# Two-layer encoder on one core: A's q features split once on 128 rows and put together by copies, V of B and C split for four heads at once, a reciprocal square root in ten steps

## The chip, the cores and the metric

The kernel runs on one core of a Trainium2 chip. The core has five engines with a program each: TensorE (PE) multiplies, VectorE (DVE) and ScalarE (ACT) work elementwise, GpSimd (POOL) helps VectorE, and SyncE (SP) does little but issue transfers. They meet by semaphores, and each runs its own program in order. The metric is the device time of one execution in microseconds (us). Results of matmuls go to PSUM, which has eight banks here, each 512 floats wide on 128 partitions; everything else lies in SBUF.

## What is computed

x is 512 tokens by 1024 features, in float32. Each of two layers does this (cut down from the reference):

```python
h = _rms_norm(x, ln1_g[l])
(a_q, a_k, a_v, b_q, b_k, b_v, c_cq, c_ckv, c_kr, gate_logits) = _split_columns(h @ w_in[l])
y_a = _gqa_axial(a_q, a_k, a_v, ...)      # A: 8 query heads, 2 key heads, 64 wide, axial rotary
y_b = _diff_attention(b_q, b_k, b_v, ...) # B: 8 heads, difference of two softmaxes, V 64 wide
y_c = _mla(c_cq, c_ckv, c_kr, ...)        # C: 8 heads from ranks 384 and 256, V 64 wide
merged = sum(sigmoid(gate_logits[n]) * (y[n] @ w_branch[l, n]) for n in range(3))
x = x + merged @ w_out[l]
x = x + relu(_rms_norm(x, ln2_g[l]) @ w_ff1[l]) ** 2 @ w_ff2[l]
```

and a last `_rms_norm` follows. In A, q and k are normalised head by head before the rotary step. In C the V of all heads is the second half of `c_kv @ w_ukv`.

## The kernel before

**Numbers in two parts.** Every operand of a matmul is held as a rounded part, *hi*, and the rest, *lo*, so that a product is two or three matmuls. `split` makes such a pair: ACT copies the source to hi (`hi`, L224), and DVE takes the source minus hi (`lo`, L227). For weights, ACT's cast gives `wh` (L61) and DVE or POOL the rest, `wl` (L67).

**Places.** Most intermediate tiles come from one pool of 25 equal SBUF places (`s4`, L201; NS4, L1233), 4 KB a partition each. A tile holds its place until the last instruction that reads it is done, and the next tile of the pool waits for that. PSUM is shared out (L1234): two banks S for scores, two T for transposes, one V for the products with V, and three L for everything else, among them `tm` (projections with tokens on the partitions), `gate` and `br`.

**Order.** `plan` writes a layer as a list of items with an estimated cost each; `weave` mixes the items of an attention with items that only need PE, and `run` (L167) goes through the list. Steps behind an item are put off by a given lag (`defer`, L147). A scheduler then lays the instructions out on the engines. SP's queue carries all the weight loads (`wr`, two buffers), in order, and the small copies in SBUF.

**The parts that the change touches.** All stand on the path of a layer in this order.

- `rsqrt` (L241): a reciprocal square root on DVE, from a bit trick and two rounds of refinement, in eleven small operations. It is called 24 times: for the norms, for A's q (`a_R`) and k (`rs`, in front of `a_kr`), for B's outputs, for C's ranks, and at the end of the kernel (`rf`, in front of `dg` and `bc`, L377).
- `a_q` (L496): a group g of four q heads. `late` (L519) transposes two heads at a time into a T bank, 128 rows by 512 tokens, and makes of it a tile `a_G` in which the first head has hi on rows 0 to 63 and lo on rows 64 to 127 of plane 0, and the second head hi on rows 64 to 127 and lo on rows 0 to 63 of plane 1. ACT writes two hi's of 64 rows, DVE two lo's of 64 rows, each half into its place. B's first transposes (`tp<-ident,b_t`) use the same two T banks.
- `v_evac` (L460), called from `b_v` (L707) and `c_v` (L905): a row tile `tt` of a projection (128 tokens, four heads of 64) comes from an L bank and is split for two heads at a time, by two calls, into two tiles; each of these holds all four row tiles of one pair of heads. A head's turn in the attention reads one such tile (`vt`, L752 and L961). `c_v(1)`, for heads 4 to 7, is woven into the heads 2 and 3 of C's attention.
- `c_pair` (L915): ACT writes q's hi into two planes by two operations of 64 by 512.
- `gate_branch` (L966): `gate` is 24 matmuls into an L bank and then DVE's `gz` (L983), which frees it; `br` is 12 into an L bank and then a DVE operation (L993 or L995).

Of the kernel before, what the change touches and what calls it, by code (L numbers as in the profile page):

```python
# [141 lines left out]
class Trunk:  # L142
    def __init__(self, tc, a, depth):
        self.tc, self.nc, self.a, self.depth = tc, tc.nc, a, depth
# [96 lines left out]
    def rsqrt(self, dst, v, n):  # L241
        v_ = self.nc.vector
        y, t, h = (self.small(f"rs{c}", n) for c in "yth")
        v_.tensor_scalar(y.bitcast(I32), v.bitcast(I32), 1, None, op0=ALU.logical_shift_right)
        v_.tensor_scalar(h, v, -0.5, None, op0=ALU.mult)
# [3 lines left out]
        v_.tensor_tensor(t, t, h, op=ALU.mult)  # L249
        v_.scalar_tensor_tensor(y, t, 1.5, y, op0=ALU.add, op1=ALU.mult)  # L250
        v_.tensor_tensor(t, y, y, op=ALU.mult)
        v_.tensor_tensor(t, t, h, op=ALU.mult)
# [207 lines left out]
    def v_evac(self, vt, tt, ps, scale):  # L460

        v = vt[:, tt].rearrange("p (a b) -> p a b", b=64)
        s = ps.rearrange("p (a b) -> p a b", b=64)
        self.hi(v[:, 0::3], s, 1.0 if scale is None else scale)
        self.lo(v[:, 1:3], s, v[:, 0::3], scale)
# [30 lines left out]
    def a_q(self, l, g):  # L496
# [22 lines left out]
        def late():  # L519
            for j in range(2):  # L520
                T = self.transpose4(st["r"], slice(j * 128, (j + 1) * 128))
                G = self.s4("a_G")
                self.hi(G[0:64, 0], T[0:64])
                self.hi(G[64:128, 1], T[64:128])
                self.lo(G[64:128, 0], T[0:64], G[0:64, 0])
                self.lo(G[0:64, 1], T[64:128], G[64:128, 1])
                self.aG[2 * g + j] = G
# [179 lines left out]
    def b_v(self, l, hb):  # L707
        def evac(tt, ps):
            if tt == 0:
                for j in range(2):  # L710
                    self.bV[2 * hb + j] = self.s4("b_V", (128, 4, 256))
            for j in range(2):
                self.v_evac(self.bV[2 * hb + j], tt, ps[:, j * 128 : (j + 1) * 128], self.rstd[:, tt : tt + 1])
# [15 lines left out]
    def att_b(self, l):  # L729
# [20 lines left out]
        def vt(h):  # L750
            o = 128 * (h % 2)
            return lambda k: self.bV[h // 2][:, k, o : o + 128]  # L752
# [152 lines left out]
    def c_v(self, l, hb):  # L905
        def evac(tt, ps):
            if tt == 0:
                for j in range(2):
                    self.cV[2 * hb + j] = self.s4("c_V", (128, 4, 256))
            for j in range(2):  # L910
                self.v_evac(self.cV[2 * hb + j], tt, ps[:, j * 128 : (j + 1) * 128], None)
# [3 lines left out]
    def c_pair(self, l, j):  # L915
# [5 lines left out]
        def q():  # L921
            ps = self.ps("L", "uq")
            self.mm(ps, self.fm_pairs(w, 0, self.want(self.cf, "q")))
            for e in range(2):
                Q = self.s4("c_Q")
                r, o = (slice(0, 64), slice(64, 128)) if e == 0 else (slice(64, 128), slice(0, 64))
                self.hi(Q[r, 0], ps[r])
                self.hi(Q[r, 1], ps[r])
# [21 lines left out]
    def att_c(self):  # L950
# [8 lines left out]
        def vt(h):  # L959
            o = 128 * (h % 2)  # L960
            return lambda k: self.cV[h // 2][:, k, o : o + 128]  # L961
# [414 lines left out]
```

## Time and profile before

| | |
|---|---|
| three runs | 1872.10, 1874.61, 1874.87 us; median 1874.61 |
| the profiled execution | 1872.25 us |
| its span, first to last instruction | 1870.4 us |
| granted clock of PE, mean | 0.993 |
| ACT, `hi` of `a_G`, 64 by 512 | 0.59 us, 16 times |
| DVE, `lo` of `a_G`, 64 by 512 | 0.69 us, 16 times |
| ACT and DVE, `b_V`, 128 by 128 | 0.37 and 0.34 us, 32 times each |
| ACT and DVE, `c_V`, 128 by 128 | 0.28 and 0.28 us, 32 times each |
| PE idle, gaps of over 0.25 us together | 39.6 us, of which 6.6 before the first matmul |

A page of the profile is one execution. Times are read from the span's start. Layer 1 runs to about 920 us, and layer 2 repeats it 921 us later: projections of A and B from 23, A's scores from 76, B's from 171, C's preparation around 324 to 341, C's scores from 340, and the second product of the feed-forward part from 644. A row of the waits says which engine and line waited for which other, for how long in all, how often, and the longest. A row of the timeline gives start, length, engine, line, what is written from what, how often, and in square brackets the idle time ahead of it and what ended it. A row of a stretch gives the busy time of PE, its weight loads, DVE, ACT and POOL, with the count of instructions, then the granted clock, the share of DMA and GB/s.

### The profile page before, as it was taken

To read this page: it belongs to the slowest core of one execution; us is meant where nothing else is said; L and a number is where in the kernel's file an instruction comes from. 1 tells how busy PE (TensorE), PEld (TensorE's weight loads), DVE (VectorE), ACT (ScalarE), POOL (GpSimd) and SP (SyncE) were. 2 spreads that over 40 slices of the span, in tenths; PEclk is the share of its full clock that TensorE was granted. 3 is DMA by queue.
4 is the path that set the end of the run, shared out by engine and by line. 5 is a ranking of instruction groups with operands and counts; after the bars stand their busy time and mean duration, and the time that the engine had idled before them with its cause. 6 is when DMAs were issued, how large, how long until landed. Compare 5 with 4: busy or idle time off the path is not lost.

```text
span 1870.4 us, 29990 instructions
## 1 busy us (share of the span) xinstructions
PE 1820.2 (97%) x10960; PEld 1603.4 (86%) x10960; DVE 1386.2 (74%) x2815; ACT 1011.1 (54%) x1852; POOL 461.6 (25%) x565
## 2 busy tenths in 40 slices
PE   8999999999999999999999999999999999999997
PEld 8998888777888898988999988878888888989897
DVE  8888889755665776867887888896566667777677
ACT  5577666655544434444446766665554444444443
POOL 4322443444101100101243224434440001011011
PEclk9999999999999999999999999999999999999998
DMA  5213331332153473745532134312232525637363
GB/s 164 79 41 85 102 108 43 96 84 81 51 170 101 100 188 92 172 121 147 138 105 68 40 91 124 92 46 84 82 91 68 163 90 125 163 94 187 100 147 94
DMA packets 85058, 197.25 MB, mean 105 GB/s; under 512 B 11952, under 2 KB 28720, under 8 KB 84912
## 3 DMA queue, kind: packets, MB, share of 16 engines
q1 hardware_dynamic: 74544, 178.56, 31.8%
q0 software_dynamic: 10368, 16.78, 6.0%
q8 instruction: 87, 1.43, 0.3%
q14 instruction: 59, 0.48, 0.1%
HBM read 174.32 MB, written 4.19 MB: 95 GB/s over the span
## 4 chain that ended last, share of the span: by engine, by line
PE 76%; DVE 12%; ACT 4%; DMA 4%; issue 2%; POOL 1%; SPq 0%; DVEq 0%; ACTq 0%; POOLq 0%
PE ff L222 18%; PE ff L1152 15%; PE gate L222 12%; PE br L222 6%; PE tm L309 5%; PE out L222 4%; PE sc L222 4%; PE pv L222 4%; PE pT L601 4%; PE c_rank L222 2%; DMA wr<-w 2%; DVE mx L585 1%; DMA fa<-wff 1%; DVE wl L67 1%; DVE p L747 1%
## 5 line engine op out<-in xcount | busy, mean ns | idle before, releaser
L67 POOL TENSOR_TENSOR wl<-wr,wh 128x256 fp32r<-128x256 f32 (+1 forms) x402 | 298.2, 772 | 534.9 <-ACT wh L61 503.1
L61 ACT CAST wh<-wr 128x1024 fp32r<-128x1024 f32 (+5 forms) x246 | 224.6, 914 | 343.2 <-PE ff L222 114.0
L1152 PE MATMUL ff<-h,fh 128*128 128x256 f32 x1792 | 324.1, 283 | 1.4 <-DVE x L1160 1.2
L222 PE MATMUL ff<-xg,wh 128*128 128x512 f32 x1024 | 315.6, 390 | 0.0
L1152 PEld LDWEIGHTS ff<-h,fh 128*128 128x128 f32 x1792 | 278.9, 192 | 3.1 <-issue 2.1
L1152 PE MATMUL ff<-h,fl 128*128 128x256 f32 x896 | 254.2, 285 | 1.5 <-DVE fl L116 1.3
L222 PE MATMUL gate<-xg,wh 128*128 128x512 f32 x768 | 241.5, 393 | 1.1 <-DVE c_K L230 1.1
L222 PEld LDWEIGHTS ff<-xg,wh 128*128 128x128 f32 x1024 | 191.7, 188 | 39.3
L115 ACT CAST fh<-fa 128x640 fp32r<-128x640 f32 (+1 forms) x144 | 108.8, 762 | 177.5 <-PE ff L1152 94.2
L309 PE MATMUL tm<-wh,xg 128*128 128x256 f32 x1024 | 202.4, 289 | 0.0
L585 DVE TENSOR_REDUCE mx<-sc 128x1 f32<-128x512 f32 x256 | 173.7, 683 | 36.7 <-PE sc L222 35.7
L222 PE MATMUL ff<-xg,wl 128*128 128x512 f32 x512 | 199.2, 389 | 0.0
L1152 PEld LDWEIGHTS ff<-h,fl 128*128 128x128 f32 x896 | 171.0, 192 | 4.7 <-DVE fl L116 4.1
L222 PEld LDWEIGHTS gate<-xg,wh 128*128 128x128 f32 x768 | 142.8, 188 | 29.9 <-PE pv L222 1.5
L309 PEld LDWEIGHTS tm<-wh,xg 128*128 128x128 f32 x1024 | 164.7, 192 | 0.2
L67 DVE TENSOR_TENSOR wl<-wr,wh 128x1024 fp32r<-128x1024 f32 (+3 forms) x117 | 134.0, 1145 | 25.2 <-ACT wh L61 25.2
L116 DVE TENSOR_TENSOR fl<-fa,fh 128x640 fp32r<-128x640 f32 (+1 forms) x144 | 124.6, 869 | 36.9 <-ACT fh L115 33.6
L222 PE MATMUL gate<-xg,wl 128*128 128x512 f32 x384 | 150.5, 392 | 0.0
L604 ACT CAST pt<-pT 128x512 fp32r<-128x512 f32 x192 | 112.0, 585 | 64.3 <-PE pT L601 62.1
L605 DVE TENSOR_TENSOR pt<-pT,pt 128x512 fp32r<-128x512 f32 x192 | 131.2, 685 | 19.3 <-ACT pt L604 17.7
L309 PE MATMUL tm<-wl,xg 128*128 128x256 f32 x512 | 145.0, 283 | 0.0
L601 PE MATMUL pT<-ident,p 128*128 128x128 f32 x768 | 116.2, 274 | 10.5 <-DVE p L595 4.8
(253 smaller groups left out, 3515.6 us busy)
## 6 DMA issues: line engine op xcount, KB each, us to landing
wr<-w SPq DMA_DIRECT2D x170, 512.0 KB, 3.6
fa<-wff SPq DMA_DIRECT2D x64, 320.0 KB, 3.4
wr<-w SPq DMA_DIRECT2D x52, 256.0 KB, 2.8
fa<-wff SPq DMA_DIRECT2D x32, 384.0 KB, 3.8
b_sq<-b_f SPq DMA_DIRECT2D x96, 64.0 KB, 2.8
b_sk<-b_f SPq DMA_DIRECT2D x96, 64.0 KB, 2.0
fa<-wff POOLq DMA_DIRECT2D x16, 320.0 KB, 4.8
fs<-wff SPq DMA_DIRECT2D x32, 160.0 KB, 2.8
```

The lines of the kernel that those rows point to most:

```text
L61: t.nc.scalar.copy(wh, self.raw)
L67: e.tensor_tensor(wl[:, q], self.raw[:, q], wh[:, q].bitcast(F32), op=ALU.subtract)
L115: t.nc.scalar.copy(a, x)
L116: t.nc.vector.tensor_tensor(b, x, a.bitcast(F32), op=ALU.subtract)
L222: self.nc.tensor.matmul(out, l, r, start=(i == 0), stop=(i == n - 1))
L309: self.nc.tensor.matmul(ps, l, r, start=(u == 0 and i == 0 and tt % 2 == 0), stop=(u == 1 and tt % 2 == 1 and i == len(p) - 1))
L585: nc.vector.tensor_reduce(m, s, axis=AX.X, op=ALU.max, negate=True)
L601: nc.tensor.transpose(T[:, k], p[:, k * 128 : (k + 1) * 128], self.ident)
L604: nc.scalar.copy(h[:, :, q], T)
L605: nc.vector.tensor_tensor(lo[:, :, q], T, h[:, :, q].bitcast(F32), op=ALU.subtract)
L747: nc.vector.scalar_tensor_tensor(p0, p1, z1, p0, op0=ALU.mult, op1=ALU.add)
L1152: nc.tensor.matmul(bk[tag], x, y, start=(new and a == 0), stop=(part[1] == n and a == len(pairs) - 1), skip_group_check=True)
```

## The change

- `rsqrt`: the operation that made -0.5 v is left out, and the two products with it become one operation each that multiplies by -0.5 and by v. Ten operations are left.
- `a_q`: ACT and DVE split all 128 rows at once into a new tile `a_P`, and four copies on SP's queue, of 64 rows by 512 (128 KB) each, put `a_G` together from it. There are 4 such tiles a layer, so 16 copies a layer. They stand behind the split, and ahead of the next weight loads, on SP's queue.
- `v_evac`: one hi and one lo per row tile, for four heads. A V tile now holds two row tiles of four heads; there are as many tiles as before, but each head reads both tiles of its four.
- `c_pair`: one operation of 64 by 1024 with a broadcast source.

```diff
--- before.py
+++ after.py
@@ -140,6 +140,9 @@
 
 
 class Trunk:
+
+    ROWS = ((0, slice(0, 64), slice(64, 128)), (1, slice(64, 128), slice(0, 64)))
+
     def __init__(self, tc, a, depth):
         self.tc, self.nc, self.a, self.depth = tc, tc.nc, a, depth
 
@@ -241,15 +244,15 @@
     def rsqrt(self, dst, v, n):
         v_ = self.nc.vector
         y, t, h = (self.small(f"rs{c}", n) for c in "yth")
+        step = lambda: v_.scalar_tensor_tensor(t, t, -0.5, v, op0=ALU.mult, op1=ALU.mult)
         v_.tensor_scalar(y.bitcast(I32), v.bitcast(I32), 1, None, op0=ALU.logical_shift_right)
-        v_.tensor_scalar(h, v, -0.5, None, op0=ALU.mult)
         v_.tensor_scalar(y.bitcast(I32), y.bitcast(I32), -1, 0x5F3759DF, op0=ALU.mult, op1=ALU.add)
 
         v_.tensor_tensor(t, y, y, op=ALU.mult)
-        v_.tensor_tensor(t, t, h, op=ALU.mult)
+        step()
         v_.scalar_tensor_tensor(y, t, 1.5, y, op0=ALU.add, op1=ALU.mult)
         v_.tensor_tensor(t, y, y, op=ALU.mult)
-        v_.tensor_tensor(t, t, h, op=ALU.mult)
+        step()
         v_.tensor_scalar(h, t, 1.5, 2.5, op0=ALU.mult, op1=ALU.add)
         v_.tensor_tensor(t, t, h, op=ALU.mult)
         v_.scalar_tensor_tensor(dst, t, 1.875, y, op0=ALU.add, op1=ALU.mult)
@@ -459,10 +462,10 @@
 
     def v_evac(self, vt, tt, ps, scale):
 
-        v = vt[:, tt].rearrange("p (a b) -> p a b", b=64)
+        v = vt[tt // 2][:, tt % 2].rearrange("p j (a u b) -> p (j a) u b", u=2, b=64)
         s = ps.rearrange("p (a b) -> p a b", b=64)
-        self.hi(v[:, 0::3], s, 1.0 if scale is None else scale)
-        self.lo(v[:, 1:3], s, v[:, 0::3], scale)
+        self.hi(v[:, :, 0], s, 1.0 if scale is None else scale)
+        self.lo(v[:, :, 1], s, v[:, :, 0], scale)
 
     def a_rope(self, tq, nh, n):
 
@@ -519,11 +522,11 @@
         def late():
             for j in range(2):
                 T = self.transpose4(st["r"], slice(j * 128, (j + 1) * 128))
-                G = self.s4("a_G")
-                self.hi(G[0:64, 0], T[0:64])
-                self.hi(G[64:128, 1], T[64:128])
-                self.lo(G[64:128, 0], T[0:64], G[0:64, 0])
-                self.lo(G[0:64, 1], T[64:128], G[64:128, 1])
+                P, G = self.s4("a_P"), self.s4("a_G")
+                self.split(P, T)
+                for e, r, o in self.ROWS:
+                    self.copy(G[r, e], P[r, 0])
+                    self.copy(G[o, e], P[r, 1])
                 self.aG[2 * g + j] = G
             norm()
 
@@ -707,10 +710,8 @@
     def b_v(self, l, hb):
         def evac(tt, ps):
             if tt == 0:
-                for j in range(2):
-                    self.bV[2 * hb + j] = self.s4("b_V", (128, 4, 256))
-            for j in range(2):
-                self.v_evac(self.bV[2 * hb + j], tt, ps[:, j * 128 : (j + 1) * 128], self.rstd[:, tt : tt + 1])
+                self.bV[hb] = [self.s4("b_V", (128, 2, 2, 256)) for _ in range(2)]
+            self.v_evac(self.bV[hb], tt, ps, self.rstd[:, tt : tt + 1])
 
         k = P_TM[f"bv{hb}"]
         return self.tm_chunk([self.big(l, k), self.big(l, k + 1)], 4, 256, "x", evac)
@@ -749,7 +750,7 @@
 
         def vt(h):
             o = 128 * (h % 2)
-            return lambda k: self.bV[h // 2][:, k, o : o + 128]
+            return lambda k: self.bV[h // 4][k // 2][:, k % 2, h // 2 % 2, o : o + 128]
 
         def finish(j, yt):
             sq = self.tmp("bsq")
@@ -905,10 +906,8 @@
     def c_v(self, l, hb):
         def evac(tt, ps):
             if tt == 0:
-                for j in range(2):
-                    self.cV[2 * hb + j] = self.s4("c_V", (128, 4, 256))
-            for j in range(2):
-                self.v_evac(self.cV[2 * hb + j], tt, ps[:, j * 128 : (j + 1) * 128], None)
+                self.cV[hb] = [self.s4("c_V", (128, 2, 2, 256)) for _ in range(2)]
+            self.v_evac(self.cV[hb], tt, ps, None)
 
         return self.tm_chunk([self.big(l, P_UV, hb * 512, 512)], 2, 256, "kv", evac)
 
@@ -924,8 +923,7 @@
             for e in range(2):
                 Q = self.s4("c_Q")
                 r, o = (slice(0, 64), slice(64, 128)) if e == 0 else (slice(64, 128), slice(0, 64))
-                self.hi(Q[r, 0], ps[r])
-                self.hi(Q[r, 1], ps[r])
+                self.hi(Q[r], ps[r].unsqueeze(1).to_broadcast([64, 2, 512]))
                 self.lo(Q[o, 0], ps[r], Q[r, 0])
                 h = 2 * j + e
                 rr = (h % 4) * 32
@@ -958,7 +956,7 @@
 
         def vt(h):
             o = 128 * (h % 2)
-            return lambda k: self.cV[h // 2][:, k, o : o + 128]
+            return lambda k: self.cV[h // 4][k // 2][:, k % 2, h // 2 % 2, o : o + 128]
 
         return self.attend(probs, vt, self.finish_plain("c"), 1.5)
```

The change also moves instructions. The rows below are from PE's program. The first place is in A's preparation, in layer 1: `tm` are B's projections, `xg` the features of x, `tp<-ident,b_t` B's transposes. Before:

```order
L309 MATMUL tm<-wh,xg_104 128x256
L309 MATMUL tm<-wl,xg_104 128x256
L309 MATMUL tm<-wh,xg_104 128x256
L338 MATMUL tp<-ident,b_t 128x128 x4
L309 MATMUL tm<-wh,xg_107 128x256
L309 MATMUL tm<-wl,xg_107 128x256
L309 MATMUL tm<-wh,xg_107 128x256
L309 MATMUL tm<-wh,xg_110 128x256
L309 MATMUL tm<-wl,xg_110 128x256
L309 MATMUL tm<-wh,xg_110 128x256
L309 MATMUL tm<-wh,xg_113 128x256
L338 MATMUL tp<-ident,b_t 128x128 x4
```

and after:

```order
L312 MATMUL tm<-wl,xg_107 128x256
L312 MATMUL tm<-wh,xg_107 128x256
L312 MATMUL tm<-wh,xg_110 128x256
L312 MATMUL tm<-wl,xg_110 128x256
L312 MATMUL tm<-wh,xg_110 128x256
L341 MATMUL tp<-ident,b_t 128x128 x4
L312 MATMUL tm<-wh,xg_97 128x256
L312 MATMUL tm<-wl,xg_97 128x256
L312 MATMUL tm<-wh,xg_97 128x256
L312 MATMUL tm<-wh,xg_104 128x256
L312 MATMUL tm<-wl,xg_104 128x256
L341 MATMUL tp<-ident,b_t 128x128 x4
```

The first group of transposes has moved six matmuls ahead, past those with xg_97 and xg_104, and the second eight.

The second place is in C's preparation: `tm<-..,c_f` are the last matmuls of C's first V, `pv` and `sc` belong to B's last heads, `tp<-ident,c_t` are the transposes of C's rotary q. Before:

```order
L222 MATMUL sc<-b_sk,b_sq 128x512 x2
L222 MATMUL pv<-pt,b_V 128x256 x7
L601 MATMUL pT<-ident,p 128x128 x4
L222 MATMUL pv<-pt,b_V 128x256
L338 MATMUL tp<-ident,c_t 128x128 x3
L222 MATMUL tm<-wh,c_f 128x256
L222 MATMUL tm<-wl,c_f 128x256
L222 MATMUL tm<-wh,c_f 128x256 x2
L222 MATMUL tm<-wl,c_f 128x256
L222 MATMUL tm<-wh,c_f 128x256
L338 MATMUL tp<-ident,c_t 128x128
```

and after:

```order
L225 MATMUL sc<-b_sk,b_sq 128x512
L225 MATMUL tm<-wh,c_f 128x256
L225 MATMUL tm<-wl,c_f 128x256
L225 MATMUL tm<-wh,c_f 128x256 x2
L225 MATMUL tm<-wl,c_f 128x256
L225 MATMUL tm<-wh,c_f 128x256
L225 MATMUL sc<-b_sk,b_sq 128x512
L225 MATMUL pv<-pt,b_V 128x256 x5
L604 MATMUL pT<-ident,p 128x128 x4
L225 MATMUL pv<-pt,b_V 128x256 x3
L341 MATMUL tp<-ident,c_t 128x128 x4
```

The six matmuls `tm` that stood between the transposes of c_t, behind `pv`, now stand ahead of `pv`; the pT between the `pv` has moved by two.

The third place is in C's attention, heads 2 and 3, at the end of `c_v(1)`: tm_5082 before and tm_5048 after are its last row tile, gate and br belong to B's branch. Before, from the end of a gate group:

```order
L222 MATMUL gate_5093<-xg1_123,wl_5028 128x512
L222 MATMUL gate_5093<-xg1_126,wh_5027 128x512 x2
L222 MATMUL gate_5093<-xg1_126,wl_5028 128x512
L222 MATMUL br_5147<-yb_3099,wh_5123 128x512 x2
L222 MATMUL br_5147<-yb_3099,wl_5124 128x512
L222 MATMUL br_5147<-yb_3607,wh_5123 128x512 x2
```

and after:

```order
L225 MATMUL gate_5057<-xg1_126,wh_4995 128x512 x2
L225 MATMUL gate_5057<-xg1_126,wl_4996 128x512
L604 MATMUL pT_5149<-ident_93,p_5105 128x128 x4
L225 MATMUL pv_5191<-pt_5002,c_V_4248 128x256
L225 MATMUL pv_5191<-pt_5003,c_V_4248 128x256
L225 MATMUL pv_5191<-pt_5002,c_V_4248 128x256
L225 MATMUL pv_5191<-pt_5003,c_V_4248 128x256
L225 MATMUL br_5111<-yb_3090,wh_5087 128x512 x2
```

Before, br follows gate at once. Afterwards four transposes and four pv stand in between, and br waits there for a DVE operation. In DVE's program the two lo's of this V tile, c_V_4983<-tm_5039 and c_V_4983<-tm_5048, now stand behind the gz of the fourth gate from there; before, those of the same row tiles stood ahead of the first gate's gz.

## The prediction

> **What bounds the kernel now.** I read the page's head and its chain first, to see which engine has to be shortened.
>
> ```profile
> span 1870.4 us, 29990 instructions
> PE 1820.2 (97%) x10960; PEld 1603.4 (86%) x10960; DVE 1386.2 (74%) x2815; ACT 1011.1 (54%) x1852; POOL 461.6 (25%) x565
> PE 76%; DVE 12%; ACT 4%; DMA 4%; issue 2%; POOL 1%; SPq 0%; DVEq 0%; ACTq 0%; POOLq 0%
> ```
>
> TensorE (PE) is busy for 97% of the span, and the change takes no matmul away and adds none. So it can shorten the time only where PE stands still or runs slowly, and lengthen it only where PE is made to wait. Saved work on ACT (54%) or DVE (74%) counts for nothing by itself. Next I read PE's waits, as us in total, times, longest, and keep those whose other end the diff touches.
>
> ```profile
> PE tp L338 <- DVE a_G L230: 4.0, 2, 2.1
> PE bc L222 <- DVE dg L377: 3.6, 1, 3.6
> PE tp L338 <- DVE a_kr L563: 2.6, 2, 1.8
> PE pv L222 <- DVE pt L605: 2.0, 2, 1.0
> PE tp L338 <- DVE c_t L894: 1.8, 2, 0.9
> ```
>
> The first row is B's transposes, held by A's q splits: 4.0 us over both layers. The second and third stand behind an rsqrt. The last two lie in C's preparation, where c_v's evacuations stand on DVE between the work that PE waits for. All five come to 14.0 us, 0.7% of the time. Then I read stretches of four us around these waits (PE, PEld, DVE, ACT, POOL busy with counts, then PEclk, the granted clock).
>
> ```profile
> 326.00:330.00 4.00, 2.38 (x17) 1.81 (x15) 4.00 (x7) 1.35 (x4) 3.07 (x2) 1.00 0.01 4
> 330.00:334.00 4.00, 3.70 (x15) 3.45 (x16) 2.63 (x9) 1.99 (x8) 0.76 (x2) 0.57 0.15 37
> 66.00:70.00 4.00, 1.88 (x16) 1.56 (x14) 3.88 (x6) 0.91 (x2) 0.00 (x0) 1.00 0.45 121
> 984.00:988.00 4.00, 2.80 (x24) 2.60 (x22) 3.82 (x10) 2.37 (x4) 1.65 (x3) 1.00 0.44 131
> 988.00:992.00 4.00, 3.34 (x17) 3.37 (x18) 2.58 (x4) 1.66 (x3) 0.00 (x0) 0.60 0.14 57
> 1248.00:1252.00 4.00, 2.08 (x15) 1.66 (x14) 4.00 (x10) 0.88 (x3) 2.47 (x2) 0.96 0.08 26
> 1252.00:1256.00 4.00, 4.00 (x17) 3.60 (x16) 2.58 (x8) 2.57 (x9) 1.16 (x2) 0.62 0.02 7
> ```
>
> Behind three of these waits the clock is down: 0.57, 0.60 and 0.62 over four us. A stretch at a clock of 0.57 does 4 x 0.57 = 2.3 us of full-speed work, so it loses 1.7 us. The stretch from 66 has the longest gap of all (PE busy 1.88 of 4) and keeps 1.00, so not every gap of this size has such a price.
>
> **The q features of A.** PE's wait in layer 1 and DVE's work before it, as start and length:
>
> ```profile
> 65.81 0.40 PE L309 MATMUL tm<-wh,xg 128*128 128x256 f32 x2
> 66.05 0.28 PE L309 MATMUL tm<-wl,xg 128*128 128x256 f32 x1
> 66.17 0.28 PE L309 MATMUL tm<-wh,xg 128*128 128x256 f32 x1
> 68.56 0.63 PE L338 MATMUL tp<-ident,b_t 128*128 128x128 f32 x4 [2.12 <-DVE a_G L230]
> ```
>
> ```profile
> 57.29 2.81 DVE L230 TENSOR_TENSOR a_G<-tp,a_G 64x512 fp32r<-64x512 f32 x4
> 60.13 1.22 DVE L493 TENSOR_REDUCE ss<-a_t 128x16 f32<-128x1024 f32 x1
> ...
> 67.03 2.81 DVE L230 TENSOR_TENSOR a_G<-tp,a_G 64x512 fp32r<-64x512 f32 x4
> 69.87 0.69 DVE L232 SCALAR_TENSOR_TENSOR b_f<-tp,b_f 128x512 fp32r<-128x512 f32 x1
> ```
>
> A bank of the transposes comes free after two lo's of 64 rows, 2.81/2 = 1.4 us. After the change it is one lo of 128 rows; b_f has that shape, 0.69. So 0.7 us goes at the bank itself. DVE also saves 2.81 - 1.38 = 1.4 us in the first group's split, but the sums at 60.13 wait for GpSimd's squares, so I let about 0.8 of it reach the second split. B's first transposes then start 1.5 us earlier, at 67.05. The order puts them six matmuls earlier, so PE arrives 6 x 0.12 us (three of them start in the 0.36 us from 65.81 to 66.17) = 0.7 us sooner, and waits from about 65.7. Those matmuls are not lost, they run behind. The gap shrinks from 2.12 to 1.35: a gain of near 0.75 us in layer 1, and a little less in layer 2, whose gap is the shorter of the two: **1.4 us** in all (0.4 to 3.0). Next late is b_t itself.
>
> The four copies per tile are new on SP's queue, and every weight load stands in that queue.
>
> ```profile
> 62.51 11.88 SPq L53 DMA_DIRECT2D wr<-w  x3
> c_K<-c_krf SPq DMA_DIRECT2D x16, 128.0 KB, 4.3
> L235 SPq DMA_DIRECT2D c_Q<-c_qr x32: 507/582/638, 337.2 to 1372.5; - x32
> L222 PE MATMUL sc<-a_K,a_G x128: 389/394/398, 76.1 to 1086.1; 128*128 128x512 f32 x128
> ```
>
> An issue of such a copy takes 0.58 us, a 128 KB one lands 4.3 us after it. The eight copies of the first group start when its second lo ends, near 58.7 at the latest, and hold SP for 8 x 0.58 = 4.6 us, to 63.3: the load behind them goes out 0.8 us later than 62.51. The second group is split by 67.03 - 0.8 + 1.38 = 67.6, issued by 72.2 and landed by 76.5; the first scores, at 76.1, read the first group, which landed by 67.6. I cost the copies at **nothing**; the cover is the two raw weight buffers and the 8 us ahead of the scores. If a load is late by those 0.8 us and PE is there, it costs up to 0.8 us at four places, 3.2 us.
>
> **The rsqrt.** The rows are those of the last one.
>
> ```profile
> 1860.01 0.17 DVE L244 TENSOR_SCALAR rsy<-var 128x2 int32<-128x2 int32 x1
> 1860.08 0.16 DVE L245 TENSOR_SCALAR rsh<-var 128x2 f32<-128x2 f32 x1
> 1860.21 0.17 DVE L246 TENSOR_SCALAR rsy<-rsy 128x2 int32<-128x2 int32 x1
> 1860.41 0.16 DVE L248 TENSOR_TENSOR rst<-rsy 128x2 f32<-128x2 f32 x1
> ```
>
> The removed step is L245. L246 needs L244, not L245, and starts 0.20 us after L244; the next step, which needs L246, also starts 0.20 after it. So a dependent step takes 0.20 whether or not L245 lies in between: the removed step ran in the shadow. Ten steps cost what eleven did: **0 us** (a gain of up to 0.13 at each of five rsqrts on the path, two ahead of a_kr in each layer and the last, 0.65). Neither the waits behind a_kr nor the one at the end will shrink.
>
> **V of C, first half.** PE and DVE at the two gaps of C's preparation:
>
> ```profile
> 327.87 0.97 PE L222 MATMUL pv<-pt,b_V 128*128 128x256 f32 x6 [1.02 <-DVE pt L605]
> 328.68 0.60 PE L601 MATMUL pT<-ident,p 128*128 128x128 f32 x4
> 329.03 0.36 PE L222 MATMUL pv<-pt,b_V 128*128 128x256 f32 x1
> 330.30 0.88 PE L338 MATMUL tp<-ident,c_t 128*128 128x128 f32 x3 [0.90 <-DVE c_t L894]
> ```
>
> ```profile
> 326.77 0.27 DVE L230 TENSOR_TENSOR c_V<-tm,c_V 128x128 fp32r<-128x128 f32 x1
> 328.40 1.75 DVE L894 TENSOR_TENSOR c_t<-c_t,c_t 128x1024 f32<-128x1024 f32 x1
> ```
>
> Today the last row tile of V stands behind tp c_t, since its bank needs both halves' evacuations, and the second half's stands behind c_t on DVE. With one evacuation for both halves, six of its matmuls (6 x 0.13 = 0.8 us, the pitch of the pv row) move ahead of the gaps; the order shows it. DVE's own chain, c_t to 330.15, stays. So 0.85 us a layer goes, **1.7 us** (1.0 to 2.6).
>
> Whether the low clock behind goes too is open: idle time in 326 to 330 falls from 1.62 to about 0.8 us. I count the price of one of the two C stretches as gone, **1.7 us** (0 to 5.1 with that at 988). [...]
>
> **V of C, second half.** One tile now holds two row tiles of four heads, not all rows of a pair. Heads 0 to 3 read both tiles to the end, so V for heads 4 to 7 finds one free place instead of two. The order shows two groups of tm whose evacuation waits until the last score of head 3. They hold two of the three L banks over eight groups of gate and br, which then take turns in one bank.
>
> ```profile
> 404.00:446.00 42.00, 42.00 (x210) 35.10 (x209) 20.25 (x43) 18.71 (x35) 19.21 (x25) 1.00 0.27 75
> ```
>
> ```profile
> 409.50 0.62 PE L222 MATMUL br<-yb,wh 128*128 128x512 f32 x2
> ```
>
> ```profile
> 409.77 0.69 DVE L983 TENSOR_TENSOR gz<-gate,rbc 128x512 f32<-128x512 f32 x1 [0.95 <-PE gate L222]
> ```
>
> PE has no gap there today, and br starts in another bank the moment gate is through, at 409.50. With one bank, br must wait for gz: 0.27 us to its start, 0.69 for itself, some 0.15 (as from the end of the second lo above, 67.03 + 1.4, to the tp at 68.56) to PE, 1.1 us. The order puts other work between, such as four pT (329.03 - 328.68 = 0.35 us) and four pv (0.54), 0.9 us, and so leaves 0.2; where one filler stands, 0.6 to 0.75. Over eight hand-overs, most of the first kind, I take 1.5 us a layer (eight of 0.2 just under), **3.0 us** in all (1.4 to 11: zero is excluded since some hand-over has less filler than 1.1, and the top is one DVE operation of 0.69 in front of each of 16). ACT and DVE keep in line behind the late evacuation, but the softmax steps stand ahead of it there.
>
> The same merging for B, and the single broadcast in c_pair, take ACT and DVE instructions away where neither is late: nothing, hidden by PE's stream (0 to 1 either way).
>
> **Sum.** The profiled execution took 1872.25 us, 2.36 under the median of the runs. 1872.25 - 1.4 - 1.7 - 1.7 + 3.0 = 1870.45; against the median 1874.61 - 1.8 = 1872.8.
>
> **Rivals.**
> - *The shared bank costs more (slower).* If DVE is at another operation at each hand-over, each of 16 costs 0.69: 11.0 us. 1874.61 - 4.8 + 11.0 = 1880.8. It decides from (3.75 + 4.8)/16 = 0.53 us a hand-over on. For it: DVE is busy for half of 404 to 446 (20.25 of 42). Against: the order has fillers at nearly all. Chance 0.16.
> - *The gaps take the low clock with them (faster).* Direct gains 2.2 and 1.7, shared bank 1.4, and all three stretches back at full speed, 5.1: 1874.61 - 7.6 = 1867.0. For it: each follows a gap that shrinks. Against: 66 to 70 shows that the link is loose. Chance 0.32.
> - *The copies make loads late.* 3.2 us on top: 1876.0; with a landing late at the scores, 1878.5. Three issues in 11.88 us, in the row of SP, speak against it: the queue has room. Chance 0.05 (slower by over the bound in most of it).
> - *The change does nothing that shows*, PE being full: 1874.6. It is held in the forecast's case.
>
> **Chances.** A measurement of this kernel can tell 0.2%, 3.75 us, from no change. The forecast's case has 0.47 and lies within it (1871 to 1878). The case of clocks lies beyond it, 0.32. The two slower cases have 0.21, of which 0.01 stays within: slower 0.20, same 0.48, faster 0.32. The range takes in the faster case and nearly all of the shared bank's up to its 0.69 a hand-over: 1866 to 1880.
>
> **What would show it.** After: tp of b_t waits for a_P about 1.4 us, the waits behind a_kr and dg stay at 2.6 and 3.6, tp c_t near 0.7, and gate and br wait for gz at 404 to 446 by 1.5 us in sum, where now PE is full. I am wrong if that stretch loses over 4 us a layer, if bc's wait is shorter by more than 0.15, or if PE waits for ACT's wh at 60 to 76.

## The result, and the profile after

| | before | after |
|---|---|---|
| four runs each, side by side, median | 1874.16 us | 1883.90 us (1881.61 to 1886.16) |
| the profiled execution | 1872.25 us | 1883.73 us |
| ratio of the times, 95% interval | | 1.0057 [1.0045, 1.0069] |
| PE idle, gaps of over 0.25 us together, to the last matmul | 39.6 us | 46.1 us |

The change makes the kernel slower by 0.57%, and the time lies above the range that I gave. The first rows of the page of the changed kernel:

```profile
span 1881.7 us, 29917 instructions
PE 1825.7 (97%) x10960; PEld 1602.3 (85%) x10960; DVE 1376.4 (73%) x2751; ACT 999.8 (53%) x1796; POOL 460.2 (24%) x565
```

DVE lost 64 instructions and 9.8 us of work, ACT 56 and 11.3 us, and PE has the same 10960 matmuls. Yet PE is busy 5.5 us longer and stands still 6.5 us more in gaps. Neither shows in the shares, which moved by a point at most. Ahead of the kernel's end, PE's clock stands at half for four windows of 3.4 us in this execution of before (at 330, 989, 1252 and 1381) and for five in that of after (two in a row from 402, one at 1286, two from 1330). Each window loses 1.7 us of work, so the clock accounts for some 1.7 of the 5.5 us; where the rest lies is not shown. PE's waits after (us in total, times, longest):

```profile
...
PE bT L777 <- DVE z L597: 4.5, 2, 2.2
PE sc L225 <- ACT p L593: 3.7, 4, 1.8
PE bc L225 <- DVE dg L380: 3.6, 1, 3.6
...
PE tp L341 <- DVE a_P L233: 2.4, 2, 1.4
PE bT L777 <- DVE bR L770: 2.3, 4, 0.9
...
PE tp L341 <- DVE a_kr L566: 1.9, 2, 1.1
...
PE tp L341 <- DVE c_t L895: 1.5, 2, 0.8
```

Most of what was forecast for the waits that the diff touches came about: tp of b_t waits 2.4 us for a_P where it waited 4.0 for a_G, tp of c_t 1.5 instead of 1.8, bc its 3.6 as before. Against the forecast, the waits for a_kr went from 2.6 to 1.9. The first row shown is new: bT, PE's transposes of the last scale factors of B (bR), now waits 2.2 us in each layer (0.18 before). The row names z, a small DVE step that ended last; what bT reads is bR, which ended just before it. The other row of bT, 2.3 us in four waits, belongs to earlier heads; with V of B alone there is much the same (2.2 in four), and that costs nothing.

To see where the time went I compare the start of the same matmul in both traces:

| first such matmul | before | after | after minus before |
|---|---|---|---|
| tp of b_t, layer 1 | 68.56 | 67.35 | -1.21 |
| uq, in C's preparation | 332.32 | 331.36 | -0.96 |
| bT | 359.12 | 359.15 | +0.03 |
| out | 544.62 | 549.82 | +5.20 |
| tp of a_kr, layer 2 | 960.22 | 965.87 | +5.65 |
| uq | 1253.72 | 1257.14 | +3.42 |
| bT | 1280.53 | 1284.94 | +4.41 |
| out | 1466.92 | 1477.88 | +10.96 |
| bc, at the end | 1862.40 | 1874.03 | +11.63 |

Up to uq the change gains in both layers, as forecast. The gain is gone at bT, and some 5 to 6.5 us a layer go between bT and out. So I read those stages: stretches of before (us, busy times of PE, PEld, DVE, ACT and POOL with counts, granted clock, DMA share, GB/s),

```profile
326.00:344.00 18.00, 15.13 (x78) 12.43 (x77) 14.21 (x29) 12.77 (x29) 8.03 (x9) 0.91 0.34 93
344.00:360.00 16.00, 15.63 (x81) 12.61 (x79) 13.21 (x38) 11.23 (x22) 5.88 (x9) 1.00 0.46 128
396.00:446.00 50.00, 48.58 (x247) 40.05 (x247) 27.31 (x58) 25.89 (x52) 21.75 (x29) 1.00 0.32 84
```

and the same stretches of after:

```profile
326.00:344.00 18.00, 16.71 (x95) 13.69 (x93) 15.21 (x28) 13.23 (x24) 9.41 (x10) 1.00 0.35 90
344.00:360.00 16.00, 12.86 (x68) 10.06 (x66) 13.92 (x34) 10.59 (x21) 5.64 (x8) 1.00 0.40 131
396.00:446.00 50.00, 47.90 (x229) 39.08 (x228) 22.77 (x45) 21.39 (x39) 21.43 (x28) 0.93 0.24 70
```

In 326 to 344 PE idles 1.29 us instead of 2.87, 1.6 us less, and the clock is up from 0.91 to 1.00, worth 18 x 0.09 = 1.6 us: together 3.2 us. Only the first half is shown to be the change's: in the traces of A's q alone and of V of B alone (below), whose gaps here are as long as in before (2.81 and 2.82 us), the clock is 1.00 too. In the next 16 us idle time goes from 0.37 to 3.14 us, and 2.8 us are lost again. From 396 to 446 PE idles 0.7 us more, and 50 x 0.07 = 3.5 us go to the clock. Layer 2 has the same three stages: gaps 1.6 us shorter from 1251, 2.7 longer from 1269, 1.3 longer from 1325 with the clock at 0.93. The loss at bT and the two parts of the loss behind 396 had to be explained.

### The profile page after: what moved, and what is told of

It reads as the page before. It is cut to its first block, busy times and chain, and to the rows that moved or that the text cites. A ratio compares the mean times of both kernels' runs of the same rounds, so it can differ in the third digit from the quotient of the medians.

```text
span 1881.7 us, 29917 instructions
## 1 busy us (share of the span) xinstructions
PE 1825.7 (97%) x10960; PEld 1602.3 (85%) x10960; DVE 1376.4 (73%) x2751; ACT 999.8 (53%) x1796; POOL 460.2 (24%) x565
## 4 chain that ended last, share of the span: by engine, by line
PE 75%; DVE 12%; ACT 5%; DMA 4%; issue 2%; POOL 1%; SPq 0%; DVEq 0%; ACTq 0%; POOLq 0%
PE ff L225 18%; PE ff L1150 13%; PE gate L225 12%; PE br L225 6%; PE tm L312 5%; PE out L225 4%; PE sc L225 4%; PE pv L225 4%; PE pT L604 4%; PE c_rank L225 3%; DMA fa<-wff 2%; DMA wr<-w 1%; ACT p L593 1%; DVE wl L67 1%; DVE fl L116 1%
## 5 line engine op out<-in xcount | busy, mean ns | idle before, releaser
L225 PE MATMUL gate<-xg,wh 128*128 128x512 f32 x768 | 245.5, 397 | 0.0
```

The source lines that it names most:

```text
L225: self.nc.tensor.matmul(out, l, r, start=(i == 0), stop=(i == n - 1))
```

## The experiments

All were run beside the kernel before; ratios are to it. "After" is the changed kernel.

### Which part carries the loss

**All but V of C.** From after, V of C goes back to two splits per row tile (`v_evac` in its old form for C):

```diff
-                self.cV[hb] = [self.s4("c_V", (128, 2, 2, 256)) for _ in range(2)]
-            self.v_evac(self.cV[hb], tt, ps, None)
+                for j in range(2):
+                    self.cV[2 * hb + j] = self.s4("c_V", (128, 4, 256))
+            for j in range(2):
+                self.v_evac(self.cV[2 * hb + j], tt, ps[:, j * 128 : (j + 1) * 128], None)
```

> All of the change but the V of C, which stays as before (tiles of a pair of heads, two operations a row tile). Theory P (places): the loss comes from C's V tiles, each held by four heads, which leave fewer places, so that C's c_K and V wait for one and ACT and DVE stand in line; then this is as fast as A's gain allows, 1871 (1869 to 1873.5), faster than before. Rival Q (the other parts: copies on SP's queue, B's V held by four heads, the rsqrt that meets GpSimd's splits): the loss stays for the most part, 1880 to 1884. Rival M (merged operations reorder the queues wherever they stand): between, 1876 to 1880.

Measured: 1875.54 us, 1.0018 [1.0009, 1.0027]. This is between the bands of P and M. About two thirds of the loss hang on V of C, and a small loss is left without it.

**V of C alone.** The same piece, the other way round, put into before.

> Before with the V of C alone changed. Theory P: the whole loss and a little more, since A's gain is missing: 1884 (1881 to 1888). Rival Q: about before, 1872 to 1876. Rival M: 1877 to 1880.

Measured: 1881.40 us, 1.0055 [1.0042, 1.0069], in the band of P. V of C alone costs what the whole change costs.

**Its layout alone.** Before, with C's V in the new tiles (two row tiles of four heads), but still two splits per row tile. This has the held places that my forecast priced, without the merged operation:

```diff
-                for j in range(2):
-                    self.cV[2 * hb + j] = self.s4("c_V", (128, 4, 256))
+                self.cV[hb] = [self.s4("c_V", (128, 2, 2, 256)) for _ in range(2)]
             for j in range(2):
-                self.v_evac(self.cV[2 * hb + j], tt, ps[:, j * 128 : (j + 1) * 128], None)
+                self.v_evac(self.cV[hb][tt // 2][:, :, j], tt % 2, ps[:, j * 128 : (j + 1) * 128], None)
```

> Before with only the layout of C's V tiles changed: two tiles of four heads, each with two row tiles, but two operations of two heads per row tile as before. Theory P: the tiles' holding is the cause, so this loses what the V of C alone loses, within 3 us: 1883 (1880 to 1887). Rival M (the merged operations and the order that they make): like before, 1873 to 1876.

Measured: 1869.53 us, 0.9983 [0.9974, 0.9991]: faster, which neither theory had. So the theory that held places make the loss fell here. The layout does cost near where I looked for it: the pv at 402, which waited 0.30 us in before, now waits

```profile
401.79 0.39 PE L222 MATMUL pv<-pt,c_V 128*128 128x256 f32 x1 [1.12 <-ACT pt L604]
```

1.12 us, and that is the last gap up to 446. But PE's largest gap of before in this part, 2.40 us at 460, is gone (below), and that outweighs it. What costs must come with the merged operation and what it moves.

**C's second half of V later.** After, with one line of the plan changed, so that `c_v(1)` is woven in behind four groups of gate and br instead of ahead of them:

```diff
-        r += weave(att[8:16], self.c_pair(l, 2) + self.c_v(l, 1) + gates(1, 4, 8))
+        r += weave(att[8:16], self.c_pair(l, 2) + gates(1, 4, 8) + self.c_v(l, 1))
```

> The whole change, but the second V of C (heads 4 to 7) stands behind the gate items of its quarter in the plan, not ahead of them, when heads 0 to 3 are nearly through with the places. Theory P: c_K finds a place and no bank is held: the loss at 399 to 412 goes, 4.5 us a layer: 1875 (1871 to 1878). Rivals Q and M: the loss stays, 1881 to 1885; also if the later V is then late for head 4.

Measured: 1863.14 us, 0.9958 [0.9946, 0.9970], far below every band. This beats both kernels, so the line is tried on before too. The gap at bT is still there, 2.25 us in both layers: what the new place mends is the stage behind 396.

**The same line in before.**

> Before with only the second V of C behind the gate items in the plan, as in the fourth run. If the new place only heals what the change broke there: as before, 1873 (1871.5 to 1875). If it is better by itself, since c_K, V and softmax steps of one moment are spread: 1866 to 1870, and then the fourth run's time says little about the change.

Measured: 1861.55 us, 0.9947 [0.9932, 0.9963], more than either theory gave. The new place is no cure of the change, it is better in itself. But the pair says something else: with `c_v(1)` out of the way, the whole change costs 0.9958 against 0.9947, no more than the intervals allow by chance, instead of 0.57%. Stretches of these two, the changed kernel with its line first:

```profile
396.00:446.00 50.00, 50.00 (x264) 42.48 (x263) 30.08 (x57) 27.60 (x50) 24.05 (x31) 1.00 0.30 91
```

```profile
396.00:446.00 50.00, 50.00 (x264) 42.60 (x263) 28.65 (x61) 27.75 (x55) 24.31 (x32) 1.00 0.33 91
```

Both have no idle time and no low clock from 396 to 446. The loss behind 396 thus needs `c_v(1)` at that place.

**The other parts alone.** Each is one piece of the change's diff, put into before: the broadcast of `c_pair`,

```diff
-                self.hi(Q[r, 0], ps[r])
-                self.hi(Q[r, 1], ps[r])
+                self.hi(Q[r], ps[r].unsqueeze(1).to_broadcast([64, 2, 512]))
```

> Before with c_pair's single broadcast alone (one ACT operation of 64 by 1024 in place of two of 64 by 512). Theory S: this edit, costed at nothing, lets DVE's order put a scaling of mx behind a lo of c_K and one of pt near 400 and 1321; ACT's p and so PE's next scores are late, by 1 to 2 us a layer instead of 0.7, with the clock at half behind it in some places: 1876 (1874 to 1880). Rival P2 (it is C's V that costs, this edit nothing): 1873 (1871 to 1874.5).

and, the other way round, after with these two lines put back:

> The whole change without c_pair's broadcast. Theory S: the gap ahead of the scores near 400 is back at 0.7 us, and what C's V costs stays: 1879 (1876 to 1881). Rival P2: as the whole change, 1882 to 1886. If the parts don't add up at all: under 1874.

then A's q features,

```diff
-                self.hi(G[0:64, 0], T[0:64])
...
+                self.split(P, T)
+                for e, r, o in self.ROWS:
...
```

> Before with A's q split on 128 rows and the copies alone. My forecast's term: gaps at the tp of b_t shrink from 2.1 and 1.9 to about 1.2, with or without the half clock behind the second: 1871.5 (1869 to 1873). Rival (copies make the loads or B's start late): 1874 to 1877.

the rsqrt,

```diff
-        v_.tensor_scalar(h, v, -0.5, None, op0=ALU.mult)
...
-        v_.tensor_tensor(t, t, h, op=ALU.mult)
+        step()
```

> Before with the ten-step rsqrt alone. My forecast's term: the step left out ran in the shadow of a dependent one: no change within 1.5 us, 1872.5 (1871 to 1874), and the wait of bc for dg stays at 3.6. Rival (each of 24 rsqrts is shorter by a step of 0.17 to 0.66): 1870 or less, bc's wait at 3.4.

and V of B:

```diff
-            for j in range(2):
-                self.v_evac(self.bV[2 * hb + j], tt, ps[:, j * 128 : (j + 1) * 128], self.rstd[:, tt : tt + 1])
+            self.v_evac(self.bV[hb], tt, ps, self.rstd[:, tt : tt + 1])
```

> Before with V of B alone changed (one hi and one lo for four heads, tiles held by four). My forecast's term: nothing, within 1.5 us: 1872.5 (1871 to 1874). Rival (B's tiles held longer make its b_s tiles or V wait, or the order of A's attention turns over): 1875 or more.

Measured:

| kernel | median, us | ratio to before |
|---|---|---|
| the broadcast alone | 1874.56 | 1.0015 [1.0004, 1.0027] |
| all but the broadcast | 1879.47 | 1.0048 [1.0031, 1.0065] |
| A's q alone | 1867.89 | 0.9981 [0.9969, 0.9993] |
| the rsqrt alone | 1874.78 | 1.0003 [0.9993, 1.0013] |
| V of B alone | 1872.29 | 0.9997 [0.9988, 1.0006] |

With V of C alone, +0.55%, the parts come to 0.15 - 0.19 + 0.03 - 0.03 + 0.55 = +0.51%, the whole to +0.57%: they add within their intervals. The rsqrt and V of B are nothing, as forecast; bc's wait in the run of the rsqrt alone, `3.6, 1, 3.6`, has not moved, though each rsqrt has one operation fewer. A's q gains more than I gave it, by the median 1 us past its band. V of C and, in small, the broadcast are the losses; the broadcast's median lies at the border of its two bands, and its interval leaves out 1 only just.

### Place 1: bT, where the gain of C's preparation goes

PE's rows of bT in layer 1, before and after:

```profile
359.12 0.63 PE L776 MATMUL bT<-ident,bR 128*128 128x128 f32 x4 [0.18 <-DVE bR L769]
```

```profile
359.15 0.63 PE L777 MATMUL bT<-ident,bR 128*128 128x128 f32 x4 [2.24 <-DVE z L597]
```

DVE's rows ahead of it in before (start, length):

```profile
354.54 0.17 DVE L766 SCALAR_TENSOR_TENSOR bv<-bss,bz 128x8 f32<-128x8 f32 x1 [0.51 <-PE bss L222]
354.74 0.72 DVE L244 TENSOR_SCALAR rsy<-bv 128x8 int32<-128x8 int32 x1
...
355.70 0.17 DVE L248 TENSOR_TENSOR rst<-rsy 128x8 f32<-128x8 f32 x1
...
358.55 0.43 DVE L769 COPY bR<-brs 128x512 f32<-128x512 f32 x1
```

and GpSimd's beside them:

```profile
351.21 4.22 POOL L67 TENSOR_TENSOR wl<-wr,wh 128x256 fp32r<-128x256 f32 x6 [5.54 <-ACT wh L61]
```

The same in after, DVE,

```profile
352.72 0.17 DVE L767 SCALAR_TENSOR_TENSOR bv<-bss,bz 128x8 f32<-128x8 f32 x1 [0.49 <-PE bss L225]
...
353.39 0.67 DVE L249 TENSOR_SCALAR rsy<-rsy 128x8 int32<-128x8 int32 x1
354.09 0.66 DVE L251 TENSOR_TENSOR rst<-rsy 128x8 f32<-128x8 f32 x1
354.78 0.66 DVE L247 SCALAR_TENSOR_TENSOR rst<-rst,bv 128x8 f32<-128x8 f32 x1
355.48 0.65 DVE L253 SCALAR_TENSOR_TENSOR rsy<-rst,rsy 128x8 f32<-128x8 f32 x1
356.16 0.65 DVE L254 TENSOR_TENSOR rst<-rsy 128x8 f32<-128x8 f32 x1
...
358.58 0.43 DVE L770 COPY bR<-brs 128x512 f32<-128x512 f32 x1
```

and GpSimd:

```profile
352.59 4.20 POOL L67 TENSOR_TENSOR wl<-wr,wh 128x256 fp32r<-128x256 f32 x6 [1.80 <-ACT wh L61]
```

PE reaches B's sums 1.8 us earlier (bv, which reads them, starts at 352.72 against 354.54), and the splits of a weight on GpSimd start 1.4 us later than in before. There the rsqrt met the end of these splits, and one step was long (0.72); now it meets them from their start, and five steps take 0.65 to 0.67 each at a pitch of 0.69, where those of before, behind the end of the splits, took 0.17 at 0.20 (from 357.26). A piece on GpSimd is 4.20/6 = 0.70 us: the pitch is as if each step waited for one piece to end. 5 x 0.49 = 2.4 us are lost, and bR ends where it did. What makes a step wait for a piece the trace does not show; it shows steps of 0.66 beside pieces of 0.70.

To show the cause and not only the coincidence, one run takes GpSimd away from this place. It is after, where ACT makes `wl` of two weights by a copy; PE's order stays as it is:

```diff
+            if getattr(self, "act", False):
+                t.nc.scalar.copy(wl, self.raw)
...
+        wg.act = wb.act = (n, d) == (1, 1)
```

> The whole change, with PE's order untouched, but the rests wl of one gate and one br weight (branch 1, tile 1) in each layer aren't computed: ACT copies the raw weight there instead, so GpSimd is idle beside B's last rsqrt (near 353 to 357 and 1279 to 1283); that part of the product is not the reference's. Theory C (beside GpSimd a small DVE step takes 0.66 us instead of 0.20): the rsqrt behind bss takes 3.6 us instead of 5.6, bT comes 1.8 us sooner and its gap of 2.24 us falls to about 0.4; PE is 1.8 us a layer ahead at 363, of which up to 1 may be lost again: 1881 (1879 to 1883). Rival (the steps wait for something else): gap and time as the whole change, 1884.

Measured: 1876.88 us, 1.0014 [1.0004, 1.0025], 7.0 us below after's median (8 by the two ratios), a larger gain than theory C gave. The rows of its rsqrt and of bT:

```profile
353.68 0.17 DVE L251 TENSOR_SCALAR rsy<-bv 128x8 int32<-128x8 int32 x1
353.88 0.18 DVE L252 TENSOR_SCALAR rsy<-rsy 128x8 int32<-128x8 int32 x1
...
357.04 0.43 DVE L773 COPY bR<-brs 128x512 f32<-128x512 f32 x1
```

```profile
357.61 0.63 PE L780 MATMUL bT<-ident,bR 128*128 128x128 f32 x4
```

The steps are back at 0.17 and bT has no gap, so the collision is the cause of it. In layer 1 bT starts 1.54 us earlier than in after, of which 0.6 is left at the start of layer 2 (tp of a_kr at 965.29 against 965.87). In layer 2 it starts at 1282.09 instead of 1284.94, and the first out comes 6.0 us earlier (1471.83 against 1477.88): there a low clock stood behind the gap, 0.74 from 1284 to 1288, and in this run it is 1.00, and where after has two windows of low clock in a row, from 1330, this run has one. So the 7 us are in two parts: PE's gaps are 42.2 us in all instead of 46.1, some 2 us a layer, and two low-clock windows fewer make 3.4 us. The mean granted clocks of all executions say the same, 0.9945 in the twelve of this kernel and 0.9927 in the four of after, 0.0018 x 1880 = 3.4 us. The gap at bT in the other kernels, layer 1: 0.18 before, 0.18 with the rsqrt alone, 0.17 with the layout alone, none without V of C, 1.80 with V of C alone, 1.76 in all but the broadcast, 2.24 after. Of the edits tried alone, only the merged split of V of C brings it.

### Place 2: the scores and V at 398 to 412

PE's first wait in the stage from 396, in before, after, and the broadcast alone:

```profile
399.70 0.73 PE L222 MATMUL sc<-c_K,c_Q 128*128 128x512 f32 x2 [0.69 <-ACT p L590]
```

```profile
401.23 0.73 PE L225 MATMUL sc<-c_K,c_Q 128*128 128x512 f32 x2 [1.56 <-ACT p L593]
```

```profile
401.24 0.73 PE L222 MATMUL sc<-c_K,c_Q 128*128 128x512 f32 x2 [2.52 <-ACT p L590]
```

These scores need a bank that the softmax `p` frees, `p` needs the scaled maximum, and DVE makes that. DVE in before,

```profile
397.94 0.21 DVE L589 TENSOR_SCALAR mx<-mx,c_rq 128x1 f32<-128x1 f32 x1
398.29 0.68 DVE L230 TENSOR_TENSOR c_K<-uk,c_K 64x512 fp32r<-64x512 f32 x1
```

and in after:

```profile
398.85 0.68 DVE L233 TENSOR_TENSOR c_K<-uk,c_K 64x512 fp32r<-64x512 f32 x1 [0.27 <-ACT c_K L228]
399.46 0.69 DVE L608 TENSOR_TENSOR pt<-pT,pt 128x512 fp32r<-128x512 f32 x1
400.07 0.20 DVE L592 TENSOR_SCALAR mx<-mx,c_rq 128x1 f32<-128x1 f32 x1
```

The scheduler has put the maximum behind two operations of 0.7 us that were behind it, and one of them, c_K, waits for ACT. With `c_v(1)` at its old place, the maximum stands behind c_K in the kernels that have the broadcast of `c_pair` (after, the broadcast alone, all but V of C, which waits 2.53 here, and the run without GpSimd at bT, 1.56), and ahead of it in the others: the wait is 0.69 with V of C alone, the layout alone, and all but the broadcast. So this wait belongs to the broadcast. With `c_v(1)` later it is gone even in the kernel that has the broadcast.

V of C has a gap of its own 3 us on. With V of C alone:

```profile
399.87 0.72 PE L222 MATMUL sc<-c_K,c_Q 128*128 128x512 f32 x2 [0.69 <-ACT p L597]
...
403.04 0.58 PE L222 MATMUL pv<-pt,c_V 128*128 128x256 f32 x1 [1.33 <-DVE c_V L230]
```

The pv wait for the merged evacuation. The layout alone waits 1.12 at this pv (above), so the merging itself adds only 0.2 us to the gap. Behind these gaps the clock falls with V of C alone, to 0.63 from 403 to 407, and in after. Stretches of after:

```profile
399.00:403.00 4.00, 2.31 (x12) 1.46 (x11) 3.35 (x8) 2.86 (x6) 0.21 (x1) 0.86 0.67 214
403.00:407.00 4.00, 3.63 (x16) 3.23 (x15) 3.22 (x8) 2.10 (x6) 0.00 (x0) 0.50 0.17 37
407.00:411.00 4.00, 4.00 (x15) 3.20 (x15) 0.95 (x2) 1.81 (x3) 2.80 (x4) 0.79 0.00 0
```

In 12 us it gives up 4 x (0.14 + 0.50 + 0.21) = 3.4 us, against gaps of 1.9 (1.56, 0.37). This is the larger half of the price, and it is loosely tied to the gaps: the layout alone, whose gaps from 398 on sum to 2.03 us (0.69, 0.22, 1.12), stays at 1.00 here. The last section sets PE's busy time beside the clock that followed.

### Place 3: 446 to 470

The stage 396 to 470 of layer 1 in all these kernels; the last column is the loss to the clock, the stretch times (1 - clock):

| kernel | idle, 396-446 | idle, 446-470 | clock |
|---|---|---|---|
| before | 1.42 | 2.45 | 0 |
| layout alone | 2.08 | 0 | 0 |
| broadcast alone | 2.53 | 2.51 | 1.5 + 1.7 |
| V of C alone | 2.29 | 3.28 | 1.5 + 1.7 |
| after | 2.10 | 2.82 | 3.5 |
| before, `c_v(1)` later | 0 | 1.18 | 0 |
| after, `c_v(1)` later | 0 | 0.90 | 0 |

The gap of before between 446 and 470 is one of 2.40 us. The rows of ACT ahead of it, in before,

```profile
454.76 1.05 ACT L61 CAST wh<-wr 128x1024 fp32r<-128x1024 f32 x1 [4.06 <-DMA wr<-w]
455.83 1.08 ACT L225 ACTIVATE c_Q<-uq 64x512 fp32r<-64x512 f32 x2
```

with V of C alone,

```profile
458.08 1.05 ACT L61 CAST wh<-wr 128x1024 fp32r<-128x1024 f32 x1 [4.39 <-DMA wr<-w]
459.15 1.08 ACT L225 ACTIVATE c_Q<-uq 64x512 fp32r<-64x512 f32 x2
```

and with the layout alone:

```profile
455.40 1.20 ACT L225 ACTIVATE c_K<-uk 64x512 fp32r<-64x512 f32 x2
456.63 0.58 ACT L614 COPY fx<-pv 64x512 f32<-64x512 f32 x1
457.23 1.05 ACT L61 CAST wh<-wr 128x1024 fp32r<-128x1024 f32 x1
```

ACT is off the path by its share (53%), but it runs in order: where the cast of a weight stands ahead of c_Q and c_K, ACT stands still for 4.06 or 4.39 us until the weight has landed, and PE's scores wait behind. With the layout alone the cast stands behind c_K, finds its weight there, and PE has no gap at all from 446 to 470. Layer 2 repeats it: before has 1.93 us there, behind a cast that waited 3.59, and the layout alone none. These 4.3 us, less the 0.8 us a layer that the layout loses at 402, are the likely source of this kernel's gain over before. I read this from the traces; no run moved the cast and nothing else.

### What can be kept

Before, with `c_v(1)` later and A's q in its new form, the two edits that gained alone:

> Before with the second V of C behind the gate items, and A's q split on 128 rows with the copies; nothing else. If the two gains lie in different stages they add: 1861.5 - 4.9 = 1856.7 (1854 to 1860). If A's gain was mainly the clock behind one gap, and that falls out otherwise here: 1859 to 1862.

Measured: 1860.42 us, 0.9924 [0.9912, 0.9937], the lowest median of all. The product of the two alone is 0.9947 x 0.9981 = 0.9928, so by the ratios they add. The time itself lies just past the band of adding and inside the rival's: that band took A's gain as 4.9 us, from medians, where the ratio gives 3.6. The interval also overlaps that of the later `c_v(1)` alone, so what A's q adds to it is not shown by this run.

## Why the prediction was wrong

**Right.** The rsqrt (1.0003 alone, bc's 3.6 us unmoved; the waits behind a_kr went from 2.6 to 1.9 in the whole change, against the forecast that they would not shrink). V of B (0.9997). The copies: A's q, which issues them, gained. The gap of A's q as such: tp b_t waits 1.6 us less, 1.4 were forecast. tp c_t: 0.75 a time, near 0.7 forecast; PE's gaps in C's preparation shrank, by 1.6 us a layer where 0.85 was forecast. Of the rivals, the one that should have ended slower, the shared bank, did not happen: after stood slower for other reasons.

**Failed: V of C.** This is the step that carries the loss. The forecast had its two halves at -1.7 - 1.7 + 3.0 = -0.4 us together; V of C alone cost 0.55%, 10 us (8 to 13). The price that it did put, 3.0 us for gate and br in turns in one bank, fell out as nothing: in after PE's gaps from 404 to 446 sum to 0.04 us, and the layout alone, which holds the places in the same way, was faster than before. The price that it left out is that of what the merged operation moves. With V of C alone that is a gap of 1.8 us a layer at bT, the 1.33 us at the pv of 403 (the layout's 1.12 among it), 3.28 us of idle time instead of 2.45 from 446 to 470, and a low clock behind these gaps.

**Failed: "nothing, hidden by PE's stream".** This was the step on the single broadcast in `c_pair`. The work saved on ACT was indeed hidden; but an operation of one shape in place of two let the scheduler put DVE's instructions in another order, and a 0.2 us step on which PE waits went behind 1.4 us of other work. Bound of the forecast 0 to 1 us; measured +0.15% alone, some 2.8 us by the ratio's middle (0.7 to 5.1). By the mean granted clock, 0.9934 in its twelve executions against 0.9953 in those of before beside them, the loss is mostly low clock behind the longer gap.

**Failed: the gain in C's preparation (1.7 us, and 1.7 of clock) taken as reaching the end.** The gap did shrink, by 1.6 us a layer. The clock term, one stretch of 1.7 us, isn't shown to be the edit's, since the stretch is at 1.00 also in runs whose gaps there are as in before. I asked what is late next inside that stretch and not 15 us on: PE arrives earlier at B's sums, and the rsqrt behind them, moved into GpSimd's splits, gives it back at bT, 2.8 us of new idle time in the next 16. The row that gave it away was in before's trace, a step of 0.72 among steps of 0.17, and I did not read it. The run without GpSimd there shows it: 7.0 us in all, about half of it gaps and half low clock.

**Failed: clocks only counted as going.** I had the stretches at 327, 988 and 1252 as prices that could fall away. They did, in this execution of the changed kernel; but new ones came behind the new gaps, at 399 to 411, 1284 to 1292 and 1328 to 1340. Each window costs some 1.7 us. Over all executions the granted clock was 0.995 in before and 0.9927 in after: some 0.002 x 1880 = 4 us of the 10. The rival that had the gaps take the low clock with them described half of this and had the wrong sign. In after the clock went to 0.50 from 403 to 407 behind 399 to 403, where PE had 2.31 us of work in four.

**Mis-sized: A's q.** 1.4 us forecast, 0.4 to 3.0; measured 0.19% alone, 3.6 us by the ratio's middle (1.3 to 5.8). The gap shrank as forecast; on top of it, its own trace has no low clock behind B's transposes at 988 nor at 330 and 1252, three windows of before. Most of that is chance of this execution: the mean granted clock was 0.9959 in its twelve and 0.9953 in those of before beside them, 1.1 us. What makes up the rest of the surplus is open.

**Open.** V of C alone against its layout alone differ by 0.72 points, some 13 us. Their two profiled executions are 10.7 us apart, with 5.1 us more idle time of PE in V of C alone and five low-clock windows against one, 6.8 us. Collision at bT, clock windows behind the gaps at 403 and 463 and their twins in layer 2, and the cast's place on ACT thus account for it by the traces, but only the first was taken out by itself, and in after. Why the merged split makes the scheduler place the cast ahead of c_Q where the layout alone places it behind was not tried.

## What to carry to other kernels

In a kernel whose bound engine is full, the work that an edit saves elsewhere counts only where that engine waits for it, and what it does to the order can count for more: read in the order of every engine which short step on the path has moved behind long ones, ahead of costing anything. Where a gain makes an engine arrive earlier, follow it to the next wait and ask what else runs there at that new time, GpSimd beside small DVE steps above all (0.66 us a step here, against 0.17). And test a part together with a change of the place where it runs: one line of the plan was worth about as much (0.53%) as the change cost (0.57%), and with it the change's loss was no longer clear of noise (0.9958 against 0.9947).

## What the runs showed of the hardware

In after, ahead of bT in layer 1, five dependent DVE steps of 128 by 8 beside GpSimd's splits took 0.65 to 0.67 us each at a pitch of 0.69, and a piece of the splits 0.70. With GpSimd idle there the same five took 0.17 or 0.18 at a pitch of 0.20 or 0.21. One of them has a single input of 8 elements a partition (`rsy<-rsy`, 0.67 and 0.18).

One ACT operation of 64 by 1024 from a broadcast source, in after,

```profile
460.66 1.02 ACT L228 ACTIVATE c_Q<-uq 64x1024 fp32r<-64x1024 f32 x1
```

took nearly what two of 64 by 512 took, 1.08 us in the row of c_Q of before above.

The granted clock was at half in stretches of 3.41 us. Between the kernel's start and end the trace of before has four of them, from 330.05, 988.82, 1251.64 and 1381.35, and that of after has one, from 1285.92, and two of twice that length, from 401.87 and 1330.29. They start a whole number of 3.413 us behind the first of their trace: 193, 270 and 308 in before, 259 and 272 in after. Counted off like this, the time of a trace falls into windows of 3.41 us, with borders that lie differently in each trace. For some of them, how long PE was busy and the clock in the next:

| kernel | window | PE busy, us of 3.41 | clock in the next window |
|---|---|---|---|
| before | 63.81 to 67.22 | 2.63 | 1.00 |
| before | 67.22 to 70.63 | 2.07 | 1.00 |
| before, `c_v(1)` later | 66.41 to 69.82 | 1.28 | 0.50 |
| before | 326.63 to 330.05 | 1.75 | 0.50 |
| rsqrt alone | 327.40 to 330.81 | 2.16 | 1.00 |
| layout alone | 399.45 to 402.86 | 2.06 | 1.00 |
| after | 398.46 to 401.87 | 1.85 | 0.50 |

The first three rows have the same gap, 2.12 and 2.13 us ahead of tp b_t: in before a border cuts it in two, in the other it lies within one window. The traces of before and after have 1059 windows at full clock from 23 us after the start to 25 us before the end. All five with PE busy for under 1.60 us were followed by half clock, none of the 1047 with 2.07 us or more, and of the seven from 1.63 to 1.85, two. So in these two traces it was in part chance whether a gap of 1.5 to 2 us was followed by a loss of another 1.7 us, and a single trace's low windows are no measure of an edit: 29 executions of before, beside one batch, had mean granted clocks from 0.993 to 0.997.
